# The modulation tiles that VectorE sums are loaded from GpSimd's queue in place of SyncE's

## The chip, the cores and the metric

The kernel runs on one core of a Trainium2 chip. The metric is the device time of one execution in microseconds; lower is better. The time before the change is the median of three runs.

## The reference

One step of a small diffusion backbone of two layers, for 128 context tokens and 128 latent tokens (width 2048), all in float32. What matters here:

```
for l in range(2):                      # for the context tokens (c_ctx) and the latent tokens (c)
    mod = silu(c) @ w_mod[l] + b_mod[l]                 # w_mod[l]: 2048 x 12288
    shift1, scale1, gate1, shift2, scale2, gate2 = split(mod, 6)
    h    = rmsnorm(x, norm1) * (1 + scale1) + shift1
    proj = h @ w_in                                     # 2048 x 4640
    mix  = concat(attention(proj), gated_linear_attention(proj)) @ w_out    # 2048 x 2048
    x    = x + gate1 * mix
    h2   = rmsnorm(x, norm2) * (1 + scale2) + shift2
    x    = x + gate2 * (relu(h2 @ w_up)**2 @ w_down)    # 2048 x 8192, 8192 x 2048
```

The six segments of `mod` are six pairs of vectors of 2048, one for the context and one for the latent tokens. Each costs a read of 16 MB of `w_mod`.

## The kernel before, in words

**Weights.** All weights are streamed from HBM once, in tiles of 512 KB. A tile of `w_in`, `w_out`, `w_up` or `w_down` (256 rows by 512 columns) is loaded by line 385 from SyncE's queue into `raw`, a pool of eight buffers. `split` then writes it as a high and a low part: ScalarE casts the high part `wh` (L109), VectorE subtracts to get the low part `wl` (L110). Three buffers of each are in rotation, and some tiles of certain blocks use other buffers under the name `wx`. TensorE makes three products of each (L409 high by high, L410 low activations by high, L411 high by low). `block` does this for one stretch of 512 output columns: eight tiles, 96 matmuls, first for the 128 context tokens (`g` = 0), then for the 128 latent ones. An MLP is 32 such blocks, four times four of `w_up` and four of `w_down`.

**Modulation.** Most segments are computed on TensorE (`mod_pe`, `mod_first`). Five are summed by VectorE in `mod_dve`: segment 5 (the MLP's gate) and segments 1, 0 and 2 of the next layer beside the first layer's MLP, and segment 5 of the second layer beside its MLP (`ON_DVE`). A segment is 32 tiles of 128 rows by 1024 columns, so there are 160 such tiles, 128 beside the first MLP and 32 beside the second. Each is loaded by line 323 into `rawm`, which uses the buffers tagged `O`. There are two of them. VectorE multiplies a tile by a column of the conditioning matrix `CT` and adds it to the sum `ga`, once for the context and once for the latent tokens: line 329, for the first tile of a half line 327. These two are called the steps of a tile here. When a segment is full, eight matmuls (L336) turn it, and for a gate the result is stored to HBM (`gd`, L193) and read back, spread over the partitions, by `gate_and_x` (`gx`, L850 and L851).

**Order.** `block` asks for the next modulation tiles while it issues its own, at `N_DVE` tiles a block (4.15 beside the first MLP). The framework then schedules each engine's instructions by a simulated timeline; the order on every engine and in every queue is fixed before the run. A DMA is issued in the order of the engine whose queue holds it, and what waits there holds up what stands behind it. SyncE's queue holds the weights' loads, GpSimd's queue the loads and stores of activations, gates and caches (`load` and `store` are both `nc.gpsimd.dma_start`, L70 and L71), and GpSimd's few element operations. A load into `rawm` waits until VectorE has done the steps on the tile two before it.

Of the kernel before, what the change touches and what calls it, by code (L numbers as in the profile page):

```python
# [20 lines left out]
P = 128  # L21
# [31 lines left out]
def trunk(tc, nc, I, O):  # L53
    with ExitStack() as st:
# [15 lines left out]
        load = nc.gpsimd.dma_start  # L70
# [5 lines left out]
        def big(tag, shape=(P, 1024), name=None, dt=F32):  # L76
            return up.tile(list(shape), dt, tag=tag, name=name or tag, bufs=BIG[tag])
# [7 lines left out]
        def mtile(shape=(P, 512), name="m"):  # L85
            return ps_m.tile(list(shape), F32, tag="m", name=name)
# [121 lines left out]
        def mod_columns(l, seg, ps, h):  # L208

            pt = mod_turn(ps)  # L210
            pv = pt.rearrange("p (h j) (c r) -> p h c j r", h=h, r=32)
            of = lambda x: x.rearrange("p (h c j) -> p h c j", h=h, c=4)
            for g in range(2):
                nc.vector.tensor_tensor(out=of(modc[l][:, seg, g]), in0=pv[:, :, :, :, g],
                                        in1=of(cols[l][:, seg * 16:seg * 16 + 16]), op=ALU.add)
            mod_finish(l, seg)
# [98 lines left out]
        def mod_dve(l, seg):  # L315
            acc = []
            for half in range(2):
                ga = [big(t, name="ga") for t in (("QT", "KT"), ("BF", "BB"))[half]]
                acc.append(ga)
                c0 = seg * D + half * 1024  # L320
                for kc in range(KC):
                    raw = big("O", name="rawm")
                    nc.sync.dma_start(raw, I["w_mod"][l, kc * P:(kc + 1) * P, c0:c0 + 1024])
                    for g in range(2):
                        c = CT[:, 2 * kc + g:2 * kc + g + 1]
                        if kc == 0:
                            nc.vector.tensor_scalar_mul(ga[g], raw, c)
                        else:
                            nc.vector.scalar_tensor_tensor(out=ga[g], in0=raw, scalar=c, in1=ga[g],  # L329
                                                           op0=ALU.mult, op1=ALU.add)  # L330
                    if half < 1 or kc < KC - 1:
                        yield 1
            ps = mtile((P, 512), "mod")
            for g in range(2):
                for q in range(4):
                    nc.tensor.matmul(ps[32 * q:32 * q + 32, :], unit[:, 1 - g:33 - g],  # L336
                                     acc[q // 2][g][:, (q % 2) * 512:(q % 2) * 512 + 512], start=g == 0, stop=g == 1)
            mod_columns(l, seg, ps, 1)
            yield 1

        def mods(todo):
            for make, *which in todo:
# [3 lines left out]
                     + [(mod_pe, l, s) for l in range(L) for s in (1, 0, 2, 4, 3, 5)  # L346
                        if (l, s) not in ON_DVE[0] + ON_DVE[1] and not (l == 0 and s < 2)])
        on_dve = [mods([(mod_dve, *x) for x in ON_DVE[i]]) for i in range(L)]
        due = [0.0, 0.0]

# [147 lines left out]
        for l in range(L):  # L498
# [381 lines left out]
            for b in range(4):  # L880
# [13 lines left out]
                for q in range(4):  # L894
                    c0 = b * D + q * 512
# [75 lines left out]
```

## Time and profile before

| | |
|---|---|
| median of 3 runs | 2385.01 us (2384.18 to 2385.63) |
| the profiled execution | 2388.39 us, its span 2386.6 us |
| TensorE busy | 2297.8 us, 96% |
| VectorE busy | 1647.6 us, 69% |
| ScalarE busy | 1090.1 us, 46% |
| GpSimd busy | 188.1 us, 8% |
| steps on modulation tiles (L329) | 378.2 us of VectorE, 300 instructions |
| moved by DMA | 613.33 MB, mean 257 GB/s |

The profile is of one execution. PE is TensorE, PEld its loading of weights, DVE is VectorE, ACT ScalarE, POOL GpSimd, SP SyncE; a q behind a name (SPq) is the engine's sequencer, which waits and issues DMAs. Names such as `rawm<-in_w_mod_dram` are what an instruction writes and reads. Matmuls overlap, so their busy times by line add up to more than the engine's. The busy share is a mean over stages of unlike kind, so a table by stage says more than the page. The first layer's MLP runs from about 526 to 1187 us, the second's from about 1640 us to the end; the 160 modulation tiles of VectorE are issued from 526.5 to 1181 and from 1630 to 1795 us.

### The profile page before, as it was taken

The page shows a single profiled execution, that of the slowest core. Times are in us where ns is not written, and L with a number is a line of the kernel's source. Part 1 is how long each engine was busy: PE and PEld are TensorE (multiplying, and loading weights), DVE is VectorE, ACT ScalarE, POOL GpSimd, SP SyncE. Part 2 cuts the span into 40 slices and gives each one's busy share as a digit, 9 for nine tenths or more (in the row PEclk, how much of TensorE's full clock was granted, in tenths as well). Part 3 has the DMA queues.
Part 4 walks back from the last instruction along what each step waited for, and adds up shares of the span by engine and source line. Part 5 has one row for each costly group of instructions (what it writes and reads, how often), then busy time and mean ns, then how long its engine had stood idle before and what let it go on. Part 6 is the DMA issues. An engine that isn't in the chain of part 4 may idle for free.

```text
span 2386.6 us, 34634 instructions
## 1 busy us (share of the span) xinstructions
PE 2297.8 (96%) x13433; PEld 1818.5 (76%) x13433; DVE 1647.6 (69%) x1971; ACT 1090.1 (46%) x1472; POOL 188.1 (8%) x259
## 2 busy tenths in 40 slices
PE   6999897999999999999999999998999999999998
PEld 3776565778878788878777777786888888888887
DVE  3665765579999999679974865566996445455455
ACT  3434434455445335435444554454554543543542
POOL 1001322100000000000000522010000000000010
PEclk9999999999999999999999999998999999999999
DMA  9999779768889889679888667776787656656664
GB/s 337 352 334 325 276 266 380 236 196 296 301 295 322 300 296 306 229 231 308 267 291 291 209 207 251 237 255 212 260 299 225 194 183 188 196 185 186 198 218 141
DMA packets 278374, 613.33 MB, mean 257 GB/s; under 512 B 24369, under 2 KB 32881, under 8 KB 278209
## 3 DMA queue, kind: packets, MB, share of 16 engines
q1 hardware_dynamic: 268128, 581.51, 72.5%
q0 software_dynamic: 9872, 29.53, 4.1%
q8 instruction: 105, 1.72, 0.3%
q14 instruction: 61, 0.49, 0.1%
q10 hardware_dynamic: 208, 0.08, 0.0%
HBM read 601.01 MB, written 10.03 MB: 256 GB/s over the span
## 4 chain that ended last, share of the span: by engine, by line
PE 84%; DVE 5%; DMA 5%; issue 3%; ACT 1%; POOL 1%; SPq 0%; DVEq 0%; POOLq 0%; ACTq 0%
PE acc L409 25%; PE acc L411 25%; PE acc L410 25%; PE mod L261 4%; DVE wl L110 2%; DVE ga L329 1%; DMA rawm<-in_w_mod_dram 1%; DMA bank<-in_w_mod_dram 1%; DMA raw<-in_w_in_dram 1%; PE aT L106 1%; DMA raw<-in_w_out_dram 1%; PE xnT L106 1%; PE sc L647 1%; PE mod L336 1%; PE po L745 0%
## 5 line engine op out<-in xcount | busy, mean ns | idle before, releaser
L110 DVE TENSOR_TENSOR wl<-raw,wh 128x1024 fp32r<-128x1024 f32 (+1 forms) x586 | 693.6, 1191 | 394.2 <-ACT wh L109 388.1
L109 ACT CAST wh<-raw 128x1024 fp32r<-128x1024 f32 (+1 forms) x586 | 592.8, 1017 | 774.0 <-PE acc L410 676.5
L409 PE MATMUL acc<-wh,TH 128*128 128x512 f32 x2248 | 892.2, 398 | 3.7 <-ACT TH L109 2.8
L410 PE MATMUL acc<-wh,TL 128*128 128x512 f32 x2248 | 883.3, 393 | 0.7 <-DVE TL L110 0.7
L411 PE MATMUL acc<-wl,TH 128*128 128x512 f32 x2248 | 865.7, 395 | 2.7 <-DVE wl L110 2.7
L409 PEld LDWEIGHTS acc<-wh,TH 128*128 128x128 f32 x2248 | 425.2, 189 | 105.2 <-issue 8.7
L411 PEld LDWEIGHTS acc<-wl,TH 128*128 128x128 f32 x2248 | 424.1, 189 | 100.0 <-DVE wl L110 5.7
L410 PEld LDWEIGHTS acc<-wh,TL 128*128 128x128 f32 x2248 | 425.1, 189 | 90.5 <-DVE TL L110 2.5
L329 DVE SCALAR_TENSOR_TENSOR ga<-rawm,CT,ga 128x1024 f32<-128x1024 f32 x300 | 378.2, 1278 | 26.5 <-DMA rawm<-in_w_mod_dram 26.1
L110 DVE TENSOR_TENSOR wx<-raw,wx 128x1024 fp32r<-128x1024 f32 (+1 forms) x182 | 194.9, 1080 | 104.1 <-ACT wx L109 103.6
L109 ACT CAST wx<-raw 128x1024 fp32r<-128x1024 f32 (+1 forms) x182 | 168.3, 938 | 192.6 <-PE acc L410 141.2
L409 PE MATMUL acc<-wx,TH 128*128 128x512 f32 x632 | 248.0, 392 | 5.4 <-ACT wx L109 5.4
L410 PE MATMUL acc<-wx,TL 128*128 128x512 f32 x632 | 247.4, 391 | 0.0
L411 PE MATMUL acc<-wx,TH 128*128 128x512 f32 x632 | 240.7, 392 | 2.0 <-DVE wx L110 2.0
L409 PEld LDWEIGHTS acc<-wx,TH 128*128 128x128 f32 x632 | 119.9, 190 | 30.8 <-ACT wx L109 5.8
L411 PEld LDWEIGHTS acc<-wx,TH 128*128 128x128 f32 x632 | 119.3, 189 | 28.4 <-DVE wx L110 2.7
L410 PEld LDWEIGHTS acc<-wx,TL 128*128 128x128 f32 x632 | 119.7, 189 | 25.1
L261 PE MATMUL mod<-bank,CT 128*32 128x256 f32 x1024 | 74.0, 414 | 17.9 <-DMA bank<-in_w_mod_dram 12.5
L193 POOL DMA_DIRECT2D gd<-gs x4 | 2.1, 523 | 867.0 <-DVE gs L192 867.0
L261 PEld LDWEIGHTS mod<-bank,CT 128*32 128x32 f32 x1024 | 32.4, 116 | 45.8 <-DMA bank<-in_w_mod_dram 15.2
L261 PE MATMUL mod<-rawm,CT 128*32 128x256 f32 x768 | 53.2, 396 | 7.5 <-DMA rawm<-in_w_mod_dram 5.3
L886 ACT ACTIVATE relu<-acc 128x512 f32<-128x512 f32 x64 | 37.9, 592 | 31.7 <-PE acc L411 31.7
(245 smaller groups left out, 1373.8 us busy)
## 6 DMA issues: line engine op xcount, KB each, us to landing
rawm<-in_w_mod_dram SPq DMA_DIRECT2D x256, 512.0 KB, 5.3
raw<-in_w_up_dram SPq DMA_DIRECT2D x256, 512.0 KB, 4.4
raw<-in_w_down_dram SPq DMA_DIRECT2D x256, 512.0 KB, 5.2
raw<-in_w_in_dram SPq DMA_DIRECT2D x144, 512.0 KB, 5.8
bank<-in_w_mod_dram SPq DMA_DIRECT2D x128, 512.0 KB, 7.5
raw<-in_w_out_dram SPq DMA_DIRECT2D x64, 512.0 KB, 7.3
gx<-gd POOLq DMA_DIRECT2D x32, 256.0 KB, 7.0
x1d<-x POOLq DMA_DIRECT2D x16, 256.0 KB, 4.1
```

The costliest lines, as they stand in the source:

```text
L106: nc.tensor.transpose(dst[:, j], s, ident)
L109: nc.scalar.copy(hi, v)
L110: nc.vector.tensor_tensor(out=lo, in0=v, in1=hi.bitcast(F32), op=ALU.subtract)
L193: store(gdram[l][seg // 3].rearrange("g (k p) -> (g k) p", p=P), gs)
L261: m = nc.tensor.matmul(ps[r:r + 32, c:c + 256], CT[:, 2 * kc:2 * kc + 32], part(raw), start=at not in seen, stop=left[at] == 0)
L329: nc.vector.scalar_tensor_tensor(out=ga[g], in0=raw, scalar=c, in1=ga[g], op0=ALU.mult, op1=ALU.add)
L336: nc.tensor.matmul(ps[32 * q:32 * q + 32, :], unit[:, 1 - g:33 - g], acc[q // 2][g][:, (q % 2) * 512:(q % 2) * 512 + 512], start=g == 0, s ...
L409: nc.tensor.matmul(acc[g], xh, wh[:, k, :], start=first, stop=False)
L410: nc.tensor.matmul(acc[g], xl, wh[:, k, :], start=False, stop=False)
L411: nc.tensor.matmul(acc[g], xh, wl[:, k, :], start=False, stop=final)
L647: nc.tensor.matmul(sps[hh][w_ * c:w_ * c + w_, n], EB[r, n % 4, j0:j0 + w_], EA[r, n % 4, i0:i0 + w_], start=True, stop=True, tile_positio ...
L886: nc.scalar.activation(r, acc, AF.Relu)
```

## The change

Line 323 issues its load with `load`, that is from GpSimd's queue, in place of SyncE's. Source, target, size and buffers stay the same.

```diff
                 for kc in range(KC):
                     raw = big("O", name="rawm")
-                    nc.sync.dma_start(raw, I["w_mod"][l, kc * P:(kc + 1) * P, c0:c0 + 1024])
+                    load(raw, I["w_mod"][l, kc * P:(kc + 1) * P, c0:c0 + 1024])
                     for g in range(2):
```

Since the scheduler orders every engine anew, more than the queue changes. On SyncE's queue, at the start of the first layer's MLP, loads of weight tiles (`raw`) and of modulation tiles (`rawm`) stood in turn:

```order
 L385 DMA raw<-in_w_out_dram 128x2x512 x16
-L385 DMA raw<-in_w_up_dram 128x2x512 x16
-L323 DMA rawm<-in_w_mod_dram 128x1024 x2
-L385 DMA raw<-in_w_up_dram 128x2x512
-L323 DMA rawm<-in_w_mod_dram 128x1024 x2
-L385 DMA raw<-in_w_up_dram 128x2x512 x2
-L323 DMA rawm<-in_w_mod_dram 128x1024
```

Now the 512 weight loads of both MLPs stand there alone, 32 of `w_up` and 32 of `w_down` in turn, with other loads only between the layers.

GpSimd's queue in the same MLP held the store of the gate (`gd`) and the loads that bring it back with the activations (`gx`), and before them the stores of the activations (`x1d`). Now the modulation tiles of the first layer stand between these:

```order
 L866 DMA x1d_3898<-x_3903 128x512
+L323 DMA rawm<-in_w_mod_dram 128x1024 x42
 L193 DMA gd_138<-gs 32x128
 L850 DMA gx<-gd_138 128x512 x2
-L851 DMA gx<-x1d_3898 128x512
-L850 DMA gx<-gd_138 128x512
-L851 DMA gx<-x1d_3898 128x512
-L850 DMA gx<-gd_138 128x512
-L851 DMA gx<-x1d_3898 128x512
+L323 DMA rawm<-in_w_mod_dram 128x1024
+L851 DMA gx<-x1d_3898 128x512
```

The first 42 modulation tiles come ahead of the gate's store, one behind the first two loads of the gate, and the other 85 behind the remaining five loads.

On VectorE, early in the first layer's MLP, the steps on modulation tiles (`ga`) and the splits (`wl`, `wx`) change places:

```order
 L329 SCALAR_TENSOR_TENSOR ga<-rawm,CT,ga 128x1024 x2
 L110 TENSOR_TENSOR wl<-raw,wh 128x1024
-L329 SCALAR_TENSOR_TENSOR ga<-rawm,CT,ga 128x1024
-L110 TENSOR_TENSOR wx<-raw,wx 128x1024
-L329 SCALAR_TENSOR_TENSOR ga<-rawm,CT,ga 128x1024 x2
+L110 TENSOR_TENSOR wx<-raw,wx 128x1024
+L329 SCALAR_TENSOR_TENSOR ga<-rawm,CT,ga 128x1024 x3
 L110 TENSOR_TENSOR wl<-raw,wh 128x1024
 L329 SCALAR_TENSOR_TENSOR ga<-rawm,CT,ga 128x1024
 L110 TENSOR_TENSOR wl<-raw,wh 128x1024
```

A step that stood between two splits now stands behind the second of them. The like happens at many places of both MLPs.

## Rows read from the trace of the kernel before

**Rows 1.** The page, busy us and share of the span by engine

```profile
PE 2297.8 (96%) x13433; PEld 1818.5 (76%) x13433; DVE 1647.6 (69%) x1971; ACT 1090.1 (46%) x1472; POOL 188.1 (8%) x259
```

**Rows 2.** Stages: length, then busy us (instructions) of five engines, PEclk, DMA share, GB/s

```profile
530.00:975.00 445.00, 443.38 (x2001) 360.91 (x2000) 422.76 (x389) 206.88 (x233) 4.26 (x8) 1.00 0.89 301
1045.00:1187.00 142.00, 142.00 (x644) 116.74 (x643) 136.34 (x127) 67.01 (x75) 0.00 (x0) 1.00 0.86 292
1650.00:1805.00 155.00, 147.12 (x655) 120.36 (x654) 140.74 (x145) 75.29 (x99) 0.00 (x0) 0.96 0.77 255
1805.00:2290.00 485.00, 485.00 (x2192) 400.15 (x2191) 238.14 (x217) 221.04 (x245) 0.00 (x0) 1.00 0.62 190
```

**Rows 3.** Waits of VectorE in 530:975, 1045:1187, 1650:1805: total, times, longest

```profile
DVE ga L329 <- DMA rawm<-in_w_mod_dram: 18.3, 21, 2.3
...
DVE ga L329 <- DMA rawm<-in_w_mod_dram: 1.5, 2, 1.3
...
DVE ga L329 <- DMA rawm<-in_w_mod_dram: 6.3, 9, 1.9
```

**Rows 4.** Waits of TensorE in 530:1187 and 1640:1680

```profile
PE acc L411 <- DVE wl L110: 1.6, 2, 1.4
...
PE acc L409 <- ACT wx L109: 5.4, 1, 5.4
PE acc L411 <- DVE wx L110: 2.0, 1, 2.0
```

**Rows 5.** Timeline of SyncE's queue, 543:555 and 700:735: start, length

```profile
544.08 0.34 SPq L323 DMA_DIRECT2D rawm<-in_w_mod_dram  x1
...
547.88 0.34 SPq L323 DMA_DIRECT2D rawm<-in_w_mod_dram  x1
...
713.15 0.34 SPq L323 DMA_DIRECT2D rawm<-in_w_mod_dram  x1
```

**Rows 6.** Timeline of VectorE, 542:555 and 715:735: start, length, [wait before it]

```profile
542.78 1.27 DVE L329 SCALAR_TENSOR_TENSOR ga<-rawm,CT,ga 128x1024 f32<-128x1024 f32 x1
543.97 1.22 DVE L110 TENSOR_TENSOR wl<-raw,wh 128x1024 fp32r<-128x1024 f32 x1
545.38 2.48 DVE L329 SCALAR_TENSOR_TENSOR ga<-rawm,CT,ga 128x1024 f32<-128x1024 f32 x2 [0.19 <-DMA rawm<-in_w_mod_dram]
...
549.51 1.28 DVE L329 SCALAR_TENSOR_TENSOR ga<-rawm,CT,ga 128x1024 f32<-128x1024 f32 x1
...
554.17 1.28 DVE L329 SCALAR_TENSOR_TENSOR ga<-rawm,CT,ga 128x1024 f32<-128x1024 f32 x1
...
733.34 2.48 DVE L329 SCALAR_TENSOR_TENSOR ga<-rawm,CT,ga 128x1024 f32<-128x1024 f32 x2 [2.33 <-DMA rawm<-in_w_mod_dram]
```

**Rows 7.** Waits of SyncE's queue, whole span

```profile
SPq L385 <- DVE wl L110: 968.0, 476, 22.1
...
SPq L323 <- DVE ga L329: 197.6, 141, 3.1
```

**Rows 8.** DMA issues in 530:975: count, KB each, median us to landing

```profile
rawm<-in_w_mod_dram SPq DMA_DIRECT2D x96, 512.0 KB, 5.2
```

**Rows 9.** DMA issues from GpSimd's queue at 1636 and at 1584.3 us

```profile
gx<-x1d POOLq DMA_DIRECT2D x1, 256.0 KB, 4.9
...
gx<-gd POOLq DMA_DIRECT2D x1, 256.0 KB, 6.9
```

**Rows 10.** Timeline of GpSimd's queue, 711:719.4

```profile
715.69 1.11 POOL L850 DMA_DIRECT2D gx<-gd  x2 [4.09 <-DMA gd<-gs]
...
718.90 0.54 POOL L851 DMA_DIRECT2D gx<-x1d  x1
```

**Rows 11.** The three loads of line L851 in 710:720

```profile
DMA to landing us min/median/max: 10.0/11.2/12.2
```

**Rows 12.** Timeline of VectorE at 1654 us

```profile
1653.96 2.48 DVE L329 SCALAR_TENSOR_TENSOR ga<-rawm,CT,ga 128x1024 f32<-128x1024 f32 x2 [0.67 <-DMA rawm<-in_w_mod_dram]
```

**Rows 13.** Stage 1660:1670, columns as in rows 2

```profile
1660.00:1670.00 10.00, 9.64 (x36) 7.74 (x36) 2.68 (x7) 0.85 (x2) 0.00 (x0) 0.74 0.20 52
```

## The prediction, made before the changed kernel ran

> **What bounds the kernel now.** I read the page first, then the table of stages, the waits of VectorE, TensorE and SyncE's queue, the timelines of SyncE's queue and of VectorE side by side, and last the landing times by queue. On the page TensorE is busy 96% of the span and VectorE 69% [rows 1], which looks like room on VectorE. The table of stages shows that there is none where it matters: from 530 to 975 us TensorE works 443.38 of 445 us at full granted clock and VectorE 422.76, 95%; from 1045 to 1187 us it is 142.00 of 142 and 136.34; from 1650 to 1805 us VectorE works 140.74 of 155. Only after 1805 us, when the summing is over, is VectorE half idle [rows 2]. So in the three stretches that hold nearly all of the 160 moved loads TensorE sets the time, with VectorE some 5% behind it. Most of those 5% is one thing: VectorE waits 18.3 us for modulation tiles in the first stretch, 1.5 in the second, 6.3 in the third, 26.1 us together [rows 3]. TensorE hardly waits for the splits of VectorE and ScalarE: 1.6 us from 530 to 1187, and 5.4 + 2.0 at the start of the second layer's MLP [rows 4].
>
> The two timelines show the loop that matters. A modulation tile has two buffers. VectorE ends the steps on a tile at 542.78 + 1.27 = 544.05, and SyncE issues the next load into that buffer at 544.08; again at 545.38 + 2.48 = 547.86 and 547.88 [rows 5, 6]. SyncE stands waiting there (197.6 us in 141 such waits, [rows 7]), so the load starts at once. The tile of 544.08 is first read at 549.51, 5.43 us later, that of 547.88 at 554.17, 6.29 us later. The median landing is 5.2 us [rows 8]. So the loop closes with little to spare, and most of each further microsecond of landing becomes a wait of VectorE, which works in order and has TensorE's splits behind it.
>
> **The change part by part.** *What goes from SyncE:* 160 issues of about 0.34 us, and the 197.6 us for which they held the queue. Behind each stood loads of MLP weights. Those have eight buffers, and SyncE spends 968.0 us waiting for a split to free one [rows 7], while TensorE waits for a split 1.6 us in 657 [rows 4]. I count this at nothing: the eight buffers hide it. If they did not, the gain could not pass the 9 us of rows 4.
>
> *What GpSimd gets:* 160 issues. One of 256 KB takes 0.54 us there [rows 10]; I take the same for 512 KB, since both have 128 rows. Its engine is otherwise nearly idle in these stretches.
>
> *How much later a tile lands.* The trace has no 512 KB load from GpSimd's queue, so I bound it. Below: a lone 256 KB load from that queue landed in 4.9 us [rows 9] where SyncE's 512 KB take 5.2 [rows 8]; were the second half of the bytes free, the tile would land 0.3 us sooner than now. Above: another 256 KB load, issued at 1584.3 us, took 6.9 us [rows 9]; with 1.1 us for the missing half (next sentence) that is 8.0, 2.8 more than now. For the missing half I read the burst at 716 us: loads of 256 KB were issued 0.54 us apart [rows 10], and every second of them, 1.08 us apart then, landed 10.0, 11.2 and 12.2 us after its issue [rows 11]; so two more take some 2.2 us, one 1.1. 4.9 + 1.1 makes 6.0 us, and with some 0.1 us until VectorE starts, 6.1. I take that, since the lone load is the nearest row in kind.
>
> *What that costs VectorE.* I paired each issue in SyncE's timeline with the step that first reads its tile (two pairs stand in rows 5 and 6). Of 94 pairs between 532.90 and 975 us, 16 are under 5.5 us long, 61 under 6.0 and 75 under 6.5. Raising each to 6.1 us adds 30.8 us there, 7.6 over the 30 pairs of the second stretch, 13.8 over 30 of the third: 52.2 us beside the 26.1 already there, 78.3. The scheduler has also moved steps of VectorE: the two steps on a tile now stand together more often, with one split more between a buffer's release and its next use. Counting the instructions between them in both orders, and pricing each from start to start (two steps take 2.48 us and one 1.28, so 1.20 a step; a split of 1.22 with the same overlap 1.14 [rows 6]), 12 of the 94 tiles have under 4.9 us of work in between, where it was 22, and the shortfall against 6.2 us shrinks by 27, 34 and 30% in the three stretches. 0.72 x 78.3 = 56.4, so 30.3 us of new waiting.
>
> *What reaches the end.* In the first stretch VectorE's lead on TensorE is used up already (TensorE's 1.6 us of waits in that layer fall there), so new waiting passes on in full. In the other two I let 3 us each be swallowed by the splits that stand ready in the three buffers: -6. *The gate store:* GpSimd's queue now holds, between the modulation tiles 42 and 44, a store of the gate, a load that waits 4.09 us for it, and six more loads [rows 10]. Tile 43, which SyncE issued at 713.15 [rows 5], follows the first two of those loads, that is 716.8, and tile 44 all seven, which landed up to 12.2 us after their issue [rows 11]. VectorE waits up to 2.33 us here now [rows 6], and I add 4. *The start of the second layer's MLP:* VectorE already waits 0.67 us for a tile there, ahead of the first splits [rows 12]: +1. Sum: 30.3 - 6 + 4 + 1 = +29 us. The profiled execution took 2388.39 us, which would become 2417.4; it lies 3.4 us over the median of the runs, 2385.01, so the forecast is 2414 us.
>
> Here the profile and the Trainium skill can be weighed. GpSimd's loads from 715.69 to 718.90 us were issued every 0.54 us in a stretch where VectorE was 95% busy [rows 10, 2]: VectorE's two-input steps did not hold up the writing of descriptors. The Trainium skill, "SBUF — State Buffer", section "SBUF: two separate sides", warns that VectorE locks GpSimd out of writing descriptors while it runs an operation in a two-port mode; the trace shows no such case here. Its page "DMA: Bandwidth & Descriptors", section "Specifications", gives about 1 us to the first byte on GpSimd's path against 0.6 on SyncE's. By that price alone a tile would land 0.4 us later and the change would cost next to nothing; the 4.9 us for half the bytes speak against it.
>
> **The rivals.** *Hidden anyway.* A tile lands at most 0.3 us later (read 5.5 us after its issue). Raising the pairs to 5.5 us adds 5.4 + 0.6 + 5.1 = 11 us; 0.72 x 37.2 = 27 us of waiting, what there is now. Time: 2384 to 2389 us. For it: the 4.9 us were taken just behind a store on the same queue, and a load that stands alone may be quicker. Against it: it was half the size.
>
> *Worse under load.* GpSimd's loads then share the DMA engines with SyncE's, which no longer stand behind them, and a tile lands at 6.9 us, as the 256 KB at 1584 us did. Raised to 7.0: 98.0 + 28.2 + 34.8 = 161 us; 0.75 x 187.1 - 26.1 = 114, less 6, plus 6: about 2499 us. Should TensorE's gaps bring down its granted clock, it would be more; against that, its wait of 1.4 us in the first stretch left the clock at 1.00 [rows 2, 4]. For this rival: 6.9 us is a row. Against it: that load had others close to it, and 4.9 us is the lone one.
>
> *Faster.* The tiles land no later than from SyncE's queue, and the new order of VectorE takes effect: its waits fall by a quarter, TensorE no longer loses the 1.6 us of rows 4 nor the 0.67 us of rows 12, and with a shorter gap at the start of the second layer's MLP the granted clock does not fall there (mean 0.74 over 9.64 us of work [rows 13], 2.5 us). That is 5 us: 2380. It decides if a tile lands within 5.2 us. Against it: there is so little that TensorE could win.
>
> **How the numbers follow.** A measurement of this kernel can tell 0.2%, 4.8 us, from no change. Forecast (a tile lands 0.5 to 1.4 us later, 2392 to 2450): 0.53. Hidden: 0.21. Worse under load: 0.19. Faster: 0.07. Slower by over 0.2% is the first and the third, 0.72; within it 0.21; faster 0.07. The range goes from 2382, which takes in the hidden case, to 2470, where the pairs are raised to 6.75 us: 77.9 + 22.0 + 28.3 = 128 us, 0.74 x 154 - 26.1 = 88, less 6, plus 4. Outside lie the faster case and most of the worse one.
>
> **What would show it.** The moved loads should show a median landing of about 6.0 us, on GpSimd's queue. VectorE's waits for modulation tiles should grow from 26.1 to some 56 us, most of it between 530 and 1000 us. TensorE should show waits for VectorE's splits of 20 us or more in the first layer's MLP, and that stretch should be longer by as much; the stages after the last moved load of each layer should take what they took. The forecast is wrong if the landing stays near 5.2 us, if VectorE's waits grow and TensorE's don't, or if an issue on GpSimd takes much more than 0.54 us.

## The result and the profile after

The changed kernel takes 2409.7 us, median of five runs, beside 2385.63 us for the kernel before; the ratio is 1.0097 (95% interval 1.0084 to 1.0109). It is slower by 24 us; the forecast was +29. The first of the five runs, which was also the profiled one, took 8139.94 us at a mean granted TensorE clock of 0.43, and neither the ratio nor anything below uses it. The profile read here is of a further run of the same kernel, beside the experiments: 2406.07 us, with a median of 2405.61 (6 runs) against 2386.43, ratio 1.0079 (1.0060 to 1.0097).

The page of that run, busy time and share by engine [rows 1]:

```profile
span 2404.3 us, 34678 instructions
PE 2303.0 (96%) x13433; PEld 1816.8 (76%) x13433; DVE 1647.0 (69%) x1971; ACT 1090.2 (45%) x1472; POOL 272.4 (11%) x419
```

VectorE works as long as before. GpSimd has 160 instructions more and 84 us. Where the 17.7 us went by which the span is longer (2404.3 against 2386.6 us) is read off by following the same weight load on SyncE's queue through both runs. The 129th, the 273rd, the 353rd and the 465th of them (near the start of the first layer's MLP, in its middle, eight loads before its last, and the first of the second layer's MLP) start, in the kernel before, at:

```profile
556.61 0.37 SPq L385 DMA_DIRECT2D raw<-in_w_up_dram  x1
...
968.02 0.37 SPq L385 DMA_DIRECT2D raw<-in_w_down_dram  x1
...
1195.87 0.37 SPq L385 DMA_DIRECT2D raw<-in_w_down_dram  x1
...
1611.28 0.37 SPq L385 DMA_DIRECT2D raw<-in_w_up_dram  x1
```

and in the changed kernel at:

```profile
558.46 0.37 SPq L385 DMA_DIRECT2D raw<-in_w_up_dram  x1
...
983.27 0.37 SPq L385 DMA_DIRECT2D raw<-in_w_down_dram  x1
...
1208.77 0.37 SPq L385 DMA_DIRECT2D raw<-in_w_down_dram  x1
...
1624.39 0.37 SPq L385 DMA_DIRECT2D raw<-in_w_up_dram  x1
```

The lag is 1.9, 15.3, 12.9 and 13.1 us. So 13.4 us are lost between 556 and 968 us, 2.4 are given back toward the end of that MLP, and hardly anything happens until the second layer's MLP. The last store of the kernel, in GpSimd's timeline, shows what is lost after that (before, then changed):

```profile
2381.42 0.54 POOL L919 DMA_DIRECT2D out_dram<-acc  x1 [0.79 <-DVE acc L916]
```

```profile
2395.22 0.54 POOL L919 DMA_DIRECT2D out_dram<-acc  x1 [0.79 <-DVE acc L916]
```

It is 13.8 us late, only 0.7 more than at 1611 us. But the span is 17.7 us longer. The other 3.9 us lie behind the last store, in the closing DRAIN of GpSimd's sequencer (the instructions of the program's end, L967: shortest, median and longest in ns; before, then changed):

```profile
L967 POOLq DRAIN  x3: 46/98/4429, 2381.4 to 2386.3; - x3
```

```profile
L967 POOLq DRAIN  x3: 46/98/8311, 2395.2 to 2404.0; - x3
```

The longest of the three begins with the last store and is what the other engines wait for at the end. It took 4.43 us and takes 8.31.

The stages, moved along by the lag [rows 2] (length, busy us of TensorE, its weight loads, VectorE, ScalarE, GpSimd; granted clock, DMA share, GB/s):

```profile
530.00:988.00 458.00, 451.15 (x2006) 362.16 (x2005) 419.91 (x386) 207.34 (x234) 54.43 (x103) 1.00 0.87 290
1059.00:1201.00 142.00, 141.96 (x642) 116.26 (x641) 134.28 (x125) 67.40 (x75) 14.78 (x28) 1.00 0.87 288
1663.00:1819.00 156.00, 147.57 (x656) 120.50 (x655) 137.90 (x143) 75.16 (x99) 15.83 (x30) 0.96 0.76 252
1819.00:2304.00 485.00, 485.00 (x2192) 400.13 (x2191) 241.01 (x219) 221.12 (x247) 0.00 (x0) 1.00 0.63 190
```

The 485 us after the last moved load hold the same 2192 matmuls. In the first stretch nearly the same work (2006 matmuls, before 2001) takes 13 us more: 5.2 of them show as idle time of TensorE (6.85 against 1.62), and 7.8 stand within its busy time. One part of these 7.8 is the granted clock, which the mean of 1.00 over so long a stretch hides. The path from a late tile to TensorE shows at 711 us: VectorE waits for a modulation tile, so the split behind its steps comes late, and TensorE waits for the split:

```profile
710.93 2.48 DVE L329 SCALAR_TENSOR_TENSOR ga<-rawm,CT,ga 128x1024 f32<-128x1024 f32 x2 [2.03 <-DMA rawm<-in_w_mod_dram]
713.33 1.22 DVE L110 TENSOR_TENSOR wl<-raw,wh 128x1024 fp32r<-128x1024 f32 x1
714.60 0.50 PE L411 MATMUL acc<-wl,TH 128*128 128x512 f32 x1 [2.17 <-DVE wl L110]
```

Behind this wait of 2.17 us the granted clock falls (columns as above; the kernel before, then the changed one):

```profile
715.00:720.00 5.00, 5.00 (x24) 4.14 (x23) 5.00 (x5) 2.27 (x4) 3.75 (x7) 1.00 0.87 287
```

```profile
715.00:720.00 5.00, 5.00 (x17) 3.94 (x16) 5.00 (x5) 1.05 (x1) 0.98 (x2) 0.66 0.89 313
```

The stretch holds 7 matmuls fewer at the same busy time, which at 0.23 us from start to start is some 1.6 us. The clock falls in this MLP also in the other four runs below that lose time there (the old order from GpSimd's queue, GpSimd with the delay, the first layer's tiles, the changed kernel with an early DRAIN), and in none of the others. The run below that has the changed kernel's order from SyncE's queue lets the two be compared matmul by matmul, from start to start. Over the 1998 that this run starts between 530 and 975 us the changed kernel takes 11.6 us more: 6.9 are idle time, 1.6 fall into the stretch of the lower clock, and 3.1 are late starts that stay under the overlap of two matmuls in the record.

VectorE's waits for modulation tiles in the first three of these stretches [rows 3]:

```profile
DVE ga L329 <- DMA rawm<-in_w_mod_dram: 32.9, 31, 3.4
DVE ga L327 <- DMA rawm<-in_w_mod_dram: 4.9, 3, 2.9
...
DVE ga L329 <- DMA rawm<-in_w_mod_dram: 6.6, 6, 2.2
...
DVE ga L329 <- DMA rawm<-in_w_mod_dram: 7.9, 7, 1.8
DVE ga L327 <- DMA rawm<-in_w_mod_dram: 0.7, 1, 0.7
```

Over the whole kernel they grew from 26.7 to 54.5 us. The loop itself, in the timelines of VectorE and of GpSimd's queue [rows 5, 6]:

```profile
539.07 1.27 DVE L329 SCALAR_TENSOR_TENSOR ga<-rawm,CT,ga 128x1024 f32<-128x1024 f32 x1
...
547.23 2.48 DVE L329 SCALAR_TENSOR_TENSOR ga<-rawm,CT,ga 128x1024 f32<-128x1024 f32 x2 [1.62 <-DMA rawm<-in_w_mod_dram]
```

```profile
540.64 0.53 POOL L323 DMA_DIRECT2D rawm<-in_w_mod_dram  x1 [4.13 <-DVE ga L329]
```

The buffer is released at 539.07 + 1.27 = 540.34, GpSimd starts the load at 540.64 and takes 0.53 us to issue it, and VectorE can read the tile only at 547.23, 6.89 us after the release. In the pair that the prediction read off for SyncE, the load began 0.03 us after the release and the tile was read 5.46 us after the release. GpSimd's load starts 0.30 us after the release nearly every time (149 of 158 times it is 0.25 to 0.35 us); where the queue is held up by something else it is more, and the mean over the 3rd to the 96th tile is 0.37.

### The profile page after: what moved, and what is told of

Same layout as the page of the kernel before. It is cut to its first block, busy times and chain, and to the rows that moved or that the text cites. A ratio compares the mean times of both kernels' runs of the same rounds, so it can differ in the third digit from the quotient of the medians.

```text
span 8138.2 us, 34678 instructions
## 1 busy us (share of the span) xinstructions
PE 8091.4 (99%) x13433; PEld 4387.8 (54%) x13433; DVE 1666.1 (20%) x1971; ACT 1102.0 (14%) x1472; POOL 253.3 (3%) x419
## 5 line engine op out<-in xcount | busy, mean ns | idle before, releaser
L409 PE MATMUL acc<-wh,TH 128*128 128x512 f32 x2248 | 2485.6, 1107 | 0.0
L410 PE MATMUL acc<-wh,TL 128*128 128x512 f32 x2248 | 2471.5, 1100 | 0.0
L411 PE MATMUL acc<-wl,TH 128*128 128x512 f32 x2248 | 2440.0, 1102 | 0.0
L409 PEld LDWEIGHTS acc<-wh,TH 128*128 128x128 f32 x2248 | 1039.0, 462 | 818.9 <-issue 801.2
L411 PEld LDWEIGHTS acc<-wl,TH 128*128 128x128 f32 x2248 | 1047.3, 466 | 800.5 <-issue 780.4
L410 PEld LDWEIGHTS acc<-wh,TL 128*128 128x128 f32 x2248 | 1053.7, 469 | 763.2 <-issue 757.2
L409 PE MATMUL acc<-wx,TH 128*128 128x512 f32 x632 | 638.1, 1010 | 4.6 <-ACT wx L109 4.6
L410 PE MATMUL acc<-wx,TL 128*128 128x512 f32 x632 | 638.4, 1010 | 0.0
L411 PE MATMUL acc<-wx,TH 128*128 128x512 f32 x632 | 625.9, 1007 | 1.4 <-DVE wx L110 1.4
L411 PEld LDWEIGHTS acc<-wx,TH 128*128 128x128 f32 x632 | 255.4, 404 | 225.0 <-issue 221.2
L409 PEld LDWEIGHTS acc<-wx,TH 128*128 128x128 f32 x632 | 256.0, 405 | 220.1 <-issue 214.7
L261 PE MATMUL mod<-bank,CT 128*32 128x256 f32 x1024 | 300.6, 1419 | 4.4 <-DVE r L123 4.4
```

Of the source, the lines that this page charges most:

```text
L261: m = nc.tensor.matmul(ps[r:r + 32, c:c + 256], CT[:, 2 * kc:2 * kc + 32], part(raw), start=at not in seen, stop=left[at] == 0)
L409: nc.tensor.matmul(acc[g], xh, wh[:, k, :], start=first, stop=False)
L410: nc.tensor.matmul(acc[g], xl, wh[:, k, :], start=False, stop=False)
L411: nc.tensor.matmul(acc[g], xh, wl[:, k, :], start=False, stop=final)
```

## Experiments

Several kernels below keep the order of another, instruction by instruction, on TensorE, VectorE and ScalarE, so that only the queue or a size differs. The order was read out of the built program and is laid down again with edges that carry no wait:

```diff
+def pin(tc, nc):
...
     with tile.TileContext(nc, **TILE) as tc:
         trunk(tc, nc, I, O)
+        pin(tc, nc)
```

`pin` puts, on each engine, every instruction of the listed order behind the one before it.

**Queue and order apart.** The scheduler had moved VectorE's steps as well as the queue. Three runs: the changed kernel again; its order with `nc.sync.dma_start` in line 323; the old order with `load`.

> The changed kernel itself, for a profile beside the others of this call. By the theory of the landing loop (a tile from GpSimd's queue lands later, VectorE waits for it, TensorE waits for VectorE's splits) the median landing of the 160 moved loads is 5.7 to 6.2 us against 5.2, VectorE's waits for modulation tiles are 45 to 65 us against 26.1, TensorE's waits for splits in the first layer's MLP 15 to 25 us against 1.6, and the time is 2407 to 2411 us. By the theory of the order (the scheduler's new order of VectorE and TensorE costs the time) the landing stays near 5.2 us and TensorE's new waits stand at places where no modulation tile is late. By the theory of freed weight loads (SyncE's loads run further ahead and crowd the DMA engines) the raw tiles and the modulation tiles both land later than before.

> The loads go from SyncE's queue as before the change, but TensorE, VectorE and ScalarE keep the order that they have in the changed kernel, instruction by instruction. Landing loop: the tiles land in 5.2 us again, the waits of VectorE are 0.72 x 26 = 19 us, and the time is 2380 to 2387 us, no slower than before. Order: 2405 to 2412 us, as the changed kernel. Freed weight loads: 2383 to 2388 us, since SyncE's queue is held up as before.

> The loads go from GpSimd's queue, but TensorE, VectorE and ScalarE keep the order that they had before the change. Landing loop: a tile lands some 0.6 to 0.8 us later than from SyncE, and without the wider spacing of the new order VectorE waits 65 to 80 us for tiles; the time is 2415 to 2435 us, slower than the changed kernel. Order: 2383 to 2389 us. Freed weight loads: 2405 to 2415 us, as the changed kernel.

Measured: 2405.61, 2387.38 (ratio 0.9998, 0.9988 to 1.0007) and 2430.0 us (1.0178, 1.0161 to 1.0195). The times came out as the landing loop has them, the first 1.4 us below its range and the second 0.4 above; the order alone costs nothing, and the old order from GpSimd's queue costs 24 us more than the new one. Two of my numbers were missed: TensorE's waits for splits in the first run (6.5 us, 15 to 25 expected) and VectorE's waits in the second (10.3 us, 19 expected). VectorE's waits over the whole kernel, for the new order from SyncE, then the old order from GpSimd:

```profile
DVE ga L329 <- DMA rawm<-in_w_mod_dram: 9.2, 15, 1.9
DVE ga L327 <- DMA rawm<-in_w_mod_dram: 1.1, 1, 1.1
```

```profile
DVE ga L329 <- DMA rawm<-in_w_mod_dram: 71.8, 61, 4.7
DVE ga L327 <- DMA rawm<-in_w_mod_dram: 5.7, 5, 2.8
```

So from SyncE 26.7 (old order) and 10.3 (new), from GpSimd 77.5 and 54.5. The scheduler's new order is worth 16 to 23 us of waiting and hides part of what the queue costs.

What the rival of the freed weight loads had named showed as well: with the order kept, the weight tiles of the first layer's MLP land 5.63 us after their issue in the mean, where it was 5.36 with the modulation tiles on SyncE's queue. The traces still tell the two apart, by the weight loads that are under way (issued and not landed) when a tile's load is issued, over the 3rd to the 96th tile. Their mean number is 1.69 in the changed kernel and 1.71 in the same order from SyncE, so the freed queue puts no more of them beside a tile. Beside one of them a tile lands after 5.23 us against 4.62, beside two after 5.85 against 5.11. A run further down, with every other tile from GpSimd, has both kinds in one execution: 4.80 us from GpSimd and 4.39 from SyncE beside one weight load, 5.90 and 5.10 beside two (9 to 34 tiles each). So the later landing goes with the queue that holds the tile's load.

**A third buffer.** It starts each load one tile earlier. To make room the weights get seven buffers in place of eight. The second run differs from the first in line 323 alone, loaded by SyncE; both keep the changed kernel's order.

```diff
-RAW_BUFS = 8
+RAW_BUFS = 7
...
-        BIG = {"QT": 1, "KT": 1, "BF": 1, "BB": 1, "ST": 2, "V": 2, "O": 2, "E": 4, "PM": 1, "KA": 1}
+        BIG = {"QT": 1, "KT": 1, "BF": 1, "BB": 1, "ST": 2, "V": 2, "O": 3, "E": 4, "PM": 1, "KA": 1}
```

> The changed kernel with three buffers for modulation tiles in place of two, and seven for the weights in place of eight to make room; TensorE, VectorE and ScalarE keep the order of the changed kernel. Landing loop: a load starts one tile (some 4.4 us) earlier, no landing of 6 us is late any more, VectorE's waits for modulation tiles fall under 8 us, and the time is 2378 to 2387 us. Order: 2405 to 2412 us. Freed weight loads: 2400 to 2412 us, since the DMA engines carry the same.

> The kernel with three buffers for modulation tiles and seven for the weights, in the order of the changed kernel, but with the tiles loaded from SyncE's queue: it differs from the run with three buffers by the queue alone. Landing loop: with three buffers no tile is late from either queue, so the two differ by the 4 us by which GpSimd's last DRAIN is longer (8.3 against 4.4 us), and this run takes 2403 to 2410 us against 2412; what both lose against before (about 20 us) is the price of the eighth weight buffer, and shows before 530 us and around 1640 us in both. A cost of GpSimd's queue that does not go through the landing (issue, descriptors, contention): this run takes 2385 to 2392 us, as the kernel before.

Measured: 2411.98 us (1.0105, 1.0089 to 1.0121) and 2407.37 us (1.0094, 1.0077 to 1.0111). My number for the first run was missed by 25 us; the theory was not, as the trace shows. VectorE waits for no modulation tile any more (the row is gone from its waits), and the first layer's MLP loses nothing. From the 129th to the 353rd weight load it takes 640.22 us, 639.26 before, 650.31 in the changed kernel. These two loads in the run with three buffers from GpSimd:

```profile
566.47 0.37 SPq L385 DMA_DIRECT2D raw<-in_w_up_dram  x1
...
1206.69 0.37 SPq L385 DMA_DIRECT2D raw<-in_w_down_dram  x1
```

The loss stands elsewhere. At the first of these loads the run is 9.9 us late; some 2.7 of them (an estimate: one tile's 12 matmuls at 0.23 us) only say that with one buffer fewer the load itself starts a tile later, so about 7 are lost ahead of that load. Another 7 are lost between the two MLPs (the lag goes from 10.8 to 17.7 us), and the last store is 15.3 us late. The run from SyncE loses nearly as much without GpSimd's queue, as expected, so this is the price of seven weight buffers in place of eight. (Its profiled execution, 2418.62 us, lies 11 us over its median, so its stages are not used here.) The medians of the two differ by 4.6 us, and their last DRAINs by 3.9 (8.31 and 4.42 us). In the run from GpSimd SyncE's weight loads are as free as in the changed kernel, and the tiles land as late (5.66 us in the mean): without VectorE's waits neither costs that MLP any time.

**The delay in doses.** GpSimd writes eight columns of the tile ahead of the load, which costs time between release and load. Once with the load from SyncE, once from GpSimd; and a third run loads every other tile from GpSimd. All three keep the changed kernel's order.

```diff
+                    nc.gpsimd.memset(raw[:, 0:8], 0.0)
                     nc.sync.dma_start(raw, I["w_mod"][l, kc * P:(kc + 1) * P, c0:c0 + 1024])
```

```diff
-                    load(raw, I["w_mod"][l, kc * P:(kc + 1) * P, c0:c0 + 1024])
+                    (load if kc % 2 else nc.sync.dma_start)(raw, I["w_mod"][l, kc * P:(kc + 1) * P, c0:c0 + 1024])
```

> The new order with the tiles loaded from SyncE's queue, as in the run that came out at 2387 us, but ahead of each load GpSimd writes zeros into eight columns of the tile (they are overwritten by the load), so that the load starts later by GpSimd's wake-up (0.30 us), the write and the step from GpSimd to SyncE: some 0.5 to 0.6 us, about what GpSimd's queue adds from a buffer's release to its landing (0.7 us). Landing loop: it does not matter from which queue the delay comes; VectorE waits 30 to 50 us for tiles against 10.3 without it, the time is 2394 to 2402 us, and the last DRAIN stays at 4.4 us. If GpSimd's queue costs by itself (descriptors, its share of the DMA engines): 2385 to 2390 us.

> The changed kernel with the same write by GpSimd ahead of each load, on the same engine, in the same order: a second dose, some 0.2 to 0.4 us more from release to landing. Landing loop: VectorE's waits rise from 54.5 to 70 to 100 us and two thirds of the rise come through, so the time is 2415 to 2435 us. If the delay is not what costs: 2404 to 2410 us, as the changed kernel.

> The changed kernel's order, with every other tile loaded from GpSimd's queue and the rest from SyncE's. Landing loop: VectorE waits about half as much more as in the changed kernel (10.3 to 54.5 us): 28 to 38 us; the time lies between 2387 and 2406 us, at 2392 to 2398 us, of which 2 us are the longer last DRAIN (6.4 us). A cost that comes of freeing SyncE's queue from waiting for VectorE would be nearly gone, since that queue still waits for every second tile: 2387 to 2390 us.

Measured: 2390.3 us (1.0012, 1.0001 to 1.0024), 2425.94 us (1.0147, 1.0126 to 1.0168) and 2385.83 us (0.9991, 0.9980 to 1.0001). The middle one is as expected. The other two cost less than I had said. The delay from SyncE was smaller than meant, 0.32 us in the mean in place of 0.5 to 0.6, and its time lies at the edge of what I had named for a cost of GpSimd's queue by itself (2385 to 2390 us); so this run does not decide between the two. Their waits of VectorE (from SyncE with the delay; every other tile):

```profile
DVE ga L330 <- DMA rawm<-in_w_mod_dram: 22.4, 21, 7.9
DVE ga L328 <- DMA rawm<-in_w_mod_dram: 1.6, 2, 1.4
```

```profile
DVE ga L329 <- DMA rawm<-in_w_mod_dram: 31.7, 33, 2.6
DVE ga L327 <- DMA rawm<-in_w_mod_dram: 2.1, 1, 2.1
```

The waits of every other tile, 33.8 us, are in the expected range, and yet the time is unchanged. That number, taken alone, would also fit the rival that blames SyncE's freed queue; the count of weight loads under way and the runs with three buffers speak against it. The table puts the kernels in the new order together. Its first column is worked out from the timelines: from the end of VectorE's second step on a tile to the landing of the load into the same buffer, the mean over the 3rd to the 96th tile. The last two are VectorE's waits for tiles and the start of the last store:

| | release to landing, us | VectorE's waits, us | last store, us |
|---|---|---|---|
| all from SyncE | 5.05 | 10.3 | 2381.90 |
| SyncE with the delay | 5.37 | 24.0 | 2385.38 |
| every other tile from GpSimd | 5.45 | 33.8 | 2381.60 |
| all from GpSimd (the change) | 5.97 | 54.5 | 2395.22 |
| first layer's from GpSimd | 5.99 | 54.9 | 2397.12 |
| GpSimd with the delay | 6.17 | 76.2 | 2417.20 |

From 5.05 to 5.45 us the waits grow by 23.5 us and the kernel hardly notices (one of the two runs in between is 3.5 us late, the other not at all). From 5.45 to 5.97 they grow by 20.7 and the last store moves by 13.6; the next 0.2 us bring 21.7 us of waits and 22.0 us of time. Against the first row, each of the three slow kernels has some 40 us of waits that never reach the end: 54.5 - 13.3 = 41.2, 54.9 - 15.2 = 39.7 and 76.2 - 35.3 = 40.9 (the old order from GpSimd's queue, against the kernel before, 77.5 - 40.4 = 37.1). So some 40 us of VectorE's waits are free in these kernels, and what goes past that comes through one for one. No run takes a tile from SyncE as late as the change does; that the same lateness would cost as much there is argued from this table, and not shown.

**Where the loss arises.** The first layer's 128 tiles from GpSimd, the second's 32 from SyncE, in the changed kernel's order.

```diff
-                    load(raw, I["w_mod"][l, kc * P:(kc + 1) * P, c0:c0 + 1024])
+                    (load if (l, seg) in ON_DVE[0] else nc.sync.dma_start)(
+                        raw, I["w_mod"][l, kc * P:(kc + 1) * P, c0:c0 + 1024])
```

> The changed kernel's order, with the 128 tiles beside the first layer's MLP loaded from GpSimd's queue and the 32 beside the second's from SyncE's. By the changed kernel's trace nearly all of the delay arises in the first layer's MLP (12.9 of 13.8 us), and the last DRAIN should take 7.5 us (128 more loads of 24 ns): 2401 to 2406 us, within 3 us of the changed kernel. If the second layer's tiles cost what the prediction gave them (some 6 us): 2397 to 2400 us.

Measured: 2401.87 us (1.0056, 1.0041 to 1.0071). The time is as expected: the first layer holds the loss, within what runs scatter (2399.75 to 2407.49). The median is 3.7 us under the changed kernel's 2405.61, of which 2.6 are a shorter last DRAIN. My number for the DRAIN was wrong; it took 5.70 us.

**The last DRAIN.** An additional `nc.gpsimd.drain()` in the second layer's MLP, in the changed kernel and in the kernel before; and 160 small loads more in the kernel before, of data that nothing uses. The order on TensorE, VectorE and ScalarE is unchanged in each.

```diff
             for b in range(4):
                 AH, AL = new_t()
+                if last and b == 3:
+                    tc.keep_in_program_order(nc.gpsimd.drain())
```

```diff
+        spare = cp.tile([16, 20], F32, tag="spare", name="spare")
...
             for b in range(4):
                 AH, AL = new_t()
+                if last and b == 1:
+                    for j in range(160):
+                        tc.keep_in_program_order(
+                            load(spare[:, j % 20:j % 20 + 1], I["w_mod"][l, 8 * j:8 * j + 16, 0:1]))
```

> The changed kernel with one DRAIN of GpSimd's queue more, in the middle of the second layer's MLP, where that queue has nothing urgent; the order on all engines is that of the changed kernel. If the last DRAIN (8.31 us in the changed kernel, 4.43 before) pays for the loads that GpSimd issued since the last one, it falls to under 1.5 us here, and the time falls by 6 to 8 us against the changed kernel, to 2399 to 2403 us. If it pays for something else (a fixed end, the landing of the last stores), it stays at 8.3 us and the time at 2405 to 2410 us.

> The kernel before with the same early DRAIN. If the last DRAIN pays for the loads issued since the one before it, it falls from 4.43 to under 1.5 us and the time by some 3 us, to 2382 to 2384 us; else nothing changes (2385 to 2388 us).

> The kernel before with 160 more loads from GpSimd's queue, of 16 rows of 4 bytes each into a tile that nothing reads, issued together early in the second layer's MLP, where that queue is idle. If the last DRAIN grows with the number of loads (24 ns each, from 8.31 - 4.43 us over 160), it takes 8.3 us and the time grows by 4 us, to 2389 to 2391 us. If it grows with their rows (2560 here, 20480 for the moved loads), it takes 4.9 us and the time stays within 1 us. A cost of issuing from GpSimd beside VectorE would show as longer VectorE steps or as waits of TensorE between 1640 and 1750 us; I expect none.

Measured: 2407.33 us (1.0092, 1.0077 to 1.0106), 2386.21 us (0.9999, 0.9989 to 1.0009) and 2390.25 us (1.0012, 1.0004 to 1.0021). The closing DRAIN of the three, in this order:

```profile
L969 POOLq DRAIN  x3: 46/93/3780, 2399.2 to 2403.5; - x3
```

```profile
L969 POOLq DRAIN  x3: 51/98/3621, 2379.7 to 2383.8; - x3
```

```profile
L973 POOLq DRAIN  x3: 46/98/7414, 2381.4 to 2389.3; - x3
```

160 loads that do nothing lengthen the DRAIN from 4.43 to 7.41 us, and their last store starts at 2381.42 as before: that part of the cost is real and has nothing to do with VectorE. An early DRAIN brings the last one from 8.31 to 3.78 us in the changed kernel and from 4.43 to 3.62 us in the one before, not under 1.5 as expected. It brought no time: in the changed kernel it stood ahead of the last four modulation tiles and lasted 9.5 us, which they waited for. That the DRAIN grows by 24 ns a load is refuted by two other runs. It took 3.33 us with every other tile from GpSimd (231 transfers on that queue), 5.70 with the first layer's (279), 4.43 before (151) and 8.31 in the change (311):

```profile
L988 POOLq DRAIN  x3: 46/98/3333, 2381.6 to 2385.4; - x3
```

It is the same within 0.02 us in runs with the same transfers on that queue (8.31 in four runs with the 311, 4.42 to 4.44 in four with the 151), so it depends on them, but by what law is left open.

No kernel here is shown to beat the one before: the early DRAIN and every other tile from GpSimd are the same within their intervals.

## Why the prediction was right, and which steps were off

**SyncE's part at nothing: right.** Without the tiles on its queue ScalarE no longer waits for weight tiles in the first layer's MLP (19.1 us before), but TensorE gained nothing by it; the loss began with that MLP.

**The issue at 0.54 us: right.** It took 0.53.

**The landing at +0.8 us: a little too much, and a term was missing.** By the rows of transfers the median went from 5.2 [rows 8] to

```profile
rawm<-in_w_mod_dram POOLq DMA_DIRECT2D x95, 512.0 KB, 5.8
```

in the first stretch, from 4.7 to 5.8 in the second, and stayed at 5.0 in the third, where the DMA engines have less to do (share 0.76). The mean over the 3rd to 96th tile went from 5.22 to 5.61 us, +0.39. The Trainium skill, "DMA: Bandwidth & Descriptors", section "Specifications", puts the first byte some 0.4 us later on GpSimd's path; the prediction held the lone load's 4.9 us against it, and the landings lie near the page's price: +0.42 us with the old order kept (5.22 to 5.64) and +0.59 with the new one (5.02 to 5.61). The first byte itself shows in no run. The conclusion that the change would then cost next to nothing did not hold. The other part of the delay was not in the sum at all: the time from release to the start of the issue, 0.37 us in the mean, where SyncE took 0.03. 5.24 became 5.97 us, +0.73 in all, close to the +0.9 with which the pairs were raised, because one part was too large and the other left out.

**VectorE's waits, 56.4 us: right, with that offset in it.** 54.5 were measured, and 77.5 in the old order, where the prediction had 78.3: the factor of 0.72 for the new order holds. By stretches, it had (18.3 + 30.8) x 0.73 = 35.8, 9.1 x 0.66 = 6.0 and 20.1 x 0.70 = 14.1; measured 37.8, 6.6 and 8.6. The third is too high: tiles land hardly later there than before (5.16 us in the mean against 5.10).

**What reaches the end: mis-sized.** I let new waiting pass on in full in the first stretch and took off 6 us for the rest. Of 18.9 us of new waits there (37.8 less 18.3 and 0.6 on the first steps of a half) 13.4 came through; of 5.1 us in the second stretch none (the lag fell by 2.4; why is not shown, and with the first layer's tiles alone from GpSimd it rose by 1.5 there), of 2.3 in the third 0.7. The premise that VectorE's lead was used up was wrong: by the doses some 40 us of waits in all never reach the end. So the loop, with the next two terms in it, gave 13.8 us where the prediction had 29, less than half.

**The gate store, +4: too much.** The wait there [rows 6] is now

```profile
729.73 2.48 DVE L329 SCALAR_TENSOR_TENSOR ga<-rawm,CT,ga 128x1024 f32<-128x1024 f32 x2 [3.37 <-DMA rawm<-in_w_mod_dram]
```

1.0 us longer.

**The granted clock: left out of the sum.** The prediction saw its fall only in the worse rival, since TensorE's wait of 1.4 us had left it at 1.00. Behind the wait of 2.17 us at 712 us it fell; that cost some 1.6 us, which are among the 13.8.

**The start of the second MLP, +1:** TensorE's wait for ScalarE went from 5.4 [rows 4] to 5.9 us.

**The end of the kernel: not thought of.** I followed GpSimd's queue to its last moved load and not to its last instruction, which every engine waits for: 3.9 us.

The sum of what was measured in the profiled run is 13.8 + 3.9 = 17.7 us, where the prediction had 29; the runs lie at +19 (2405.61 against 2386.43) and +24 (2409.7 against 2385.63). What lies between the profiled run and the median of the first result has no profile of its own. The direction, the place and the mechanism hold. That the size came out so near is in part luck: the loop was put at twice its size, and the DRAIN, which was left out, filled some of the difference.

**What I had named as a sign** was TensorE waiting 20 us or more for splits in the first MLP. It shows 6.5 in that MLP:

```profile
PE acc L411 <- DVE wl L110: 6.5, 6, 2.2
```

The rest is in the busy time, as the stages show. The longer stretch was the sign to name.

**The rivals.** A tile landed 0.4 to 0.6 us later, which is neither the 0.3 us at most of the hidden case nor the 6.9 us after issue of the worse one. The faster case needed a gain from the new order; from SyncE's queue that order took 2387.38 us against 2386.43.

## What to carry to other kernels

A load that is issued only when its buffer comes free closes a loop: release, start of the issue, landing, first use. Compare that loop with the work that the consumer has in between before moving the load to another queue; here the first 0.4 us more were free, the next 0.5 moved the last store by 14 us, and 0.2 us on top of that by 22. A third buffer takes the loop away, if the room does not come from something that needs it more.

## What the runs showed of the hardware

GpSimd's queue starts a waiting load 0.30 us after VectorE's release, SyncE's 0.03 us. Beside the same number of weight loads under way, a tile of 512 KB from GpSimd's queue lands 0.4 to 0.8 us later after its issue than one from SyncE's. The DRAIN of GpSimd at the program's end takes 3.3 to 8.3 us, depending on the transfers that its queue has issued, and every engine waits for it. Not all that TensorE loses is in its waits; part is in its busy time, which was 451.15 us for 2006 matmuls where 2001 took 443.38: late starts under the overlap of two matmuls, and a granted clock of 0.66 from 715 to 720 us, behind a wait of 2.17 us.
